# Two-layer attention block: modulation with raw fp32 weights stationary, and its chunks moved

## The chip, the cores and the metric

One core of one Trainium2 chip runs one launch of the kernel. The metric is the device time of the launch in microseconds (us). Everything below is fp32 work: a product is made either from fp32r (reduced precision) high and low parts, or from plain fp32 operands.

## The reference

Two blocks follow each other. The first has an AB layer (latent attention and grouped-query attention) and a CD layer (window attention and a short convolution), over 512 tokens of width 1024 with a context of 256 tokens. The second has an even and an odd layer. Only the first block has the modulation that is changed here:

```python
sc, scc = jax.nn.silu(c), jax.nn.silu(c_ctx)          # [1024] each
for i in range(2):                                    # the AB layer, the CD layer
    mod   = sc  @ mod_w[i] + mod_b[i]                 # mod_w[i]: [1024, 3072]
    mod_c = scc @ mod_w[i] + mod_b[i]
    # shift, scale, gate = three parts of 1024
    # h = rmsnorm(x) * (1 + scale) + shift ;  x = x + gate * (mix @ w_out)
```

So each layer multiplies a 1024 x 3072 matrix by two vectors (one for the tokens, one for the context). Shift and scale are needed before the layer's input projections, the gate only at its output projection.

## The kernel before

The weights of each layer's modulation are laid out as 12 chunks of 256 columns, 1 MB each: chunks 0 to 3 are the shift, 4 to 7 the scale, 8 to 11 the gate. A chunk arrives as two loads of 512 KB. With two layers there are 24 chunks.

*A chunk before.* ScalarE casts each 128x512 quarter of the chunk to its high part and VectorE subtracts for the low part: four casts and four subtractions. TensorE holds the vectors stationary (`sc4`, 128x4: high and low parts of the two vectors) and streams the weights: 16 matmuls of 256 columns. The result is a row block, [4, 256]. A second pair of small fp32 matmuls (L348, stationary [5, 128], two columns moving) turns rows into per-feature columns, sums the high and low parts and adds the bias. The gates stay rows: they are spilled, summed with two matmuls of 512 columns (`gate_sum`, L361), spilled again, and broadcast over the partitions by a DMA (`gate_bc`, L368).

*Where the chunks run.* The eight shift and scale chunks of layer 0 run in `start` (L641), which also normalises and transposes the tokens; their loads rotate through four buffers (`mraw`). `ab_first` (L690), the first projection, takes each feature block as it is finished. The eight shift and scale chunks of layer 1 (`mods`) and the four gate chunks of layer 0 run among the projections of the AB layer (latents, queries, gates). The four gate chunks of layer 1 run as fillers inside the window attention of the CD layer.

*Order.* The kernel is written for a tile framework. The order in which functions are traced gives priority; the framework then lays out each engine's instruction list ahead of time, with a timeline of its own, so that work that is ready fills gaps. Tiles of one name rotate through a fixed number of buffers in trace order: `raw` has three of 512 KB, shared by all weight loads. `pace` (L613) spreads units of filler work over the items of an attention; `hook` ties work to one item. All weight loads and most spills are issued from SP's queue. PSUM bank F is single: projections, modulation and, late in the grouped-query attention, attention outputs use it in turn.

Of the kernel before, what the change touches and what calls it, by code (L numbers as in the profile page):

```python
# [9 lines left out]
F32 = mybir.dt.float32  # L10
# [19 lines left out]
class Kern:  # L30
# [69 lines left out]
    def setup(self, stack):  # L100
# [8 lines left out]
        self.grow_d, self.gsum_d = ([self.dram.tile([n, 1024], F32, name=f"g{n}row{l}_d") for l in range(2)] for n in (5, 2))  # L109
# [6 lines left out]
        self.sel2 = c.tile([5, 2], F32, name="sel2")  # L116
        nc.scalar.dma_start(out=self.sel2, in_=I["sel"])
# [17 lines left out]
    def rstd(self, ms, n):  # L135
        """ms [128, n] mean squares -> (ms + eps)^-0.5"""
# [4 lines left out]
    def split(self, src, hi, lo):  # L141
        """hi, lo (fp32r) of a fp32 AP (PSUM or SBUF)"""
# [16 lines left out]
    def silu2(self, ps, out):  # L159
        """out = 2*silu(ps)"""  # L160
# [4 lines left out]
    def head_norm(self, ps, H, d):  # L165
        """ps PSUM [128, T, H*d] -> normalised fp32 SBUF [128, T, H, d] (no gain)"""
# [18 lines left out]
    def rope(self, out, xn, C, S, r0, rot):  # L185
        """out = xn*C plus the rotary part on [r0, r0+rot), half-split pairs; C [128, T, d], S [128, T, rot]"""
# [12 lines left out]
    def gain_heads(self, out, xn, g):  # L199
        """out = xn*g over [128, T, H, d]"""  # L200
# [9 lines left out]
    def weights(self, ap):  # L210
        """ap DRAM [128, nk, n] -> [(k0, hi, lo)] pieces in fp32r"""
# [48 lines left out]
    def proj_feat(self, out, X, W, c0, t0, n):  # L260
        """feature-major block: out PSUM [128, n] = W[:, c0:c0+128]^T @ X[:, t0:t0+n]"""
# [20 lines left out]
    def feat(self, X, W, t=512):  # L282
        """feature blocks of a chunk over t tokens: yields (b, PSUM [128, n], t0, n)"""
# [9 lines left out]
    def load_silu_c(self):  # L293
# [7 lines left out]
        self.split(self.sc, self.sc4[:, :, 0:2], self.sc4[:, :, 2:4])  # L301

    def mod_load(self, layer, ch, pool):
        """the loads of a mod chunk, ahead of mod_first"""
        rows = self.tl(pool, [5, 256], "rows", 4)
        self.nc.scalar.dma_start(out=rows[4:5, :], in_=self.I["mod_b"][layer:layer + 1, 256 * ch:256 * ch + 256])
        raws = []
        for k in (0, 4):
            raws.append(self.tl(pool, [128, 4, 256], "mraw", 4))
            self.nc.sync.dma_start(out=raws[-1], in_=self.I["mod_w"][layer, ch][:, k:k + 4, :])  # L310
        return rows, raws

    def mod_first(self, ld, pool):
        """rows [5, 256] (x, ctx hi parts, lo parts, bias) of a loaded mod chunk"""
        nc = self.nc
        rows, raws = ld
        p = self.B()
        for kk in range(8):
            if kk % 2 == 0:
                hi, lo = (self.tl(pool, [128, 2, 256], x, 5, F32R) for x in ("mhi", "mlo"))  # L320
                self.split(raws[kk // 4][:, kk % 4:kk % 4 + 2, :], hi, lo)
            for j, w in enumerate((hi, lo)):
                nc.tensor.matmul(out=p[0:4, 0:256], lhsT=self.sc4[:, kk, :], rhs=w[:, kk % 2, :], start=kk + j == 0,
                                 stop=kk == 7 and j == 1)
        nc.vector.tensor_copy(out=rows[0:4, :], in_=p[0:4, 0:256])
        return rows, self.sel2

    def mod_rows(self, layer, ch):
        """rows [5, 256] (x, ctx hi parts, lo parts, bias) of mod chunk ch"""
        nc = self.nc  # L330
        W = self.weights(self.I["mod_w"][layer, ch])
        rows = self.T4([5, 256])
        nc.scalar.dma_start(out=rows[4:5, :], in_=self.I["mod_b"][layer:layer + 1, 256 * ch:256 * ch + 256])
        p = self.B()
        for k0, hi, lo in W:
            for k in range(hi.shape[1]):
                kk = k0 + k
                nc.tensor.matmul(out=p[0:4, 0:256], lhsT=self.sc4[:, kk, :], rhs=hi[:, k, :], start=kk == 0, stop=False)
                nc.tensor.matmul(out=p[0:4, 0:256], lhsT=self.sc4[:, kk, :], rhs=lo[:, k, :], start=False, stop=kk == 7)
        nc.vector.tensor_copy(out=rows[0:4, :], in_=p[0:4, 0:256])  # L340
        return rows, self.sel2

    def mod_cols(self, layer, ch, rs):
        """per-feature columns modT[layer][:, 2*ch + b, (x, ctx)]; the scales with one added"""
        rows, sel = rs
        p = self.B()
        for b in range(2):
            self.nc.tensor.matmul(out=p[:, 2 * b:2 * b + 2], lhsT=rows[:, 128 * b:128 * b + 128], rhs=sel)  # L348
        self.nc.vector.tensor_scalar(out=self.modT[layer][:, 2 * ch:2 * ch + 2, :].rearrange("p b e -> p (b e)"),
                                     in0=p[:, 0:4], scalar1=1.0, scalar2=1.0 if ch >= 4 else 0.0,  # L350
                                     op0=ALU.mult, op1=ALU.add)

    def gate_rows(self, layer, chs):
        """rows [5, 256] of the gate's chunks, spilled"""
        for h in chs:
# [1486 lines left out]
```

## Time and profile before

| | |
|---|---|
| time, median of 3 runs | 1550.29 us (1546.9 to 1552.76) |
| profiled execution, span of its instructions | 1546.3 us |
| TensorE (PE) busy | 1486.4 us, 96% |
| weight loads of TensorE (PEld) busy | 1373.0 us, 89% |
| VectorE (DVE) busy | 1036.5 us, 67% |
| ScalarE (ACT) busy | 846.5 us, 55% |
| GpSimd (POOL) busy | 546.9 us, 35% |
| HBM read and written | 144.06 MB and 22.28 MB |

The profile shows one execution, of which only the span is given, not a time of its own: the runs lie 0.6 to 6.5 us above the span, the median 4.0. Busy time of PE counts the modelled end of each matmul, so neighbours overlap. PEclk is the granted TensorE clock as a share of full speed: 1.00 is 2.4 GHz and 0.50 is 1.2 GHz. L followed by a number is a line of the kernel.

### The profile page before, as it was taken

The numbers are of one execution on the slowest core, as the hardware profiler recorded it, in microseconds if no ns is written. First come the engines' busy times: TensorE is split into PE (matmuls) and PEld (weight loads), VectorE is DVE, ScalarE is ACT, GpSimd is POOL, SyncE is SP. The second block draws the span as 40 slices with busy tenths as digits, with TensorE's granted clock in tenths as the row PEclk, the third lists the DMA queues.
The fourth block names the chain that finished last, engine by engine and source line by source line (L and its number), as shares of the span: only waits on it lengthen the run. The fifth ranks groups of instructions, "written<-read, shape, count | busy, mean of one in ns | idle before, by whom it ended". The sixth has DMA issues, their size and how long they took to land.

```text
span 1546.3 us, 28606 instructions
## 1 busy us (share of the span) xinstructions
PE 1486.4 (96%) x10760; PEld 1373.0 (89%) x10760; DVE 1036.5 (67%) x2121; ACT 846.5 (55%) x1759; POOL 546.9 (35%) x652
## 2 busy tenths in 40 slices
PE   6899999989999999999999999999999999999998
PEld 3799788877998999888889889998899999998998
DVE  6777887889886477777755458986544465565444
ACT  6545555689996154565643446557433544455322
POOL 1533533567674033232421434444201334443000
PEclk8999999999999999999999999999999999999999
DMA  8344564121221332322234222124334321223423
GB/s 304 121 128 120 183 203 162 45 103 33 63 70 31 146 121 71 101 96 86 93 115 145 80 96 82 66 86 137 116 103 143 119 94 57 82 69 132 148 90 110
DMA packets 60685, 168.20 MB, mean 109 GB/s; under 512 B 9890, under 2 KB 18530, under 8 KB 60546
## 3 DMA queue, kind: packets, MB, share of 16 engines
q1 hardware_dynamic: 54768, 163.52, 31.8%
q10 hardware_dynamic: 5778, 2.84, 0.7%
q8 instruction: 85, 1.39, 0.4%
q14 instruction: 54, 0.44, 0.1%
HBM read 144.06 MB, written 22.28 MB: 108 GB/s over the span
## 4 chain that ended last, share of the span: by engine, by line
PE 79%; DVE 8%; DMA 5%; ACT 3%; issue 2%; POOL 2%; SPq 0%; ACTq 0%; DVEq 0%; POOLq 0%
PE A L240 17%; PE A L238 17%; PE A L239 17%; PE B L524 3%; PE F L238 3%; PE F L239 3%; PE F L240 3%; PE F L595 2%; PE B L238 2%; PE B L239 2%; PE B L240 2%; DVE wl L232 1%; PE B L996 1%; PE B L388 1%; PE B L1168 1%
## 5 line engine op out<-in xcount | busy, mean ns | idle before, releaser
L229 ACT CAST wh<-raw 128x512 fp32r<-128x512 f32 (+1 forms) x388 | 232.4, 616 | 237.8 <-PE A L240 166.9
L232 DVE TENSOR_TENSOR wl<-raw,wh 128x512 fp32r<-128x512 f32 (+1 forms) x320 | 233.4, 744 | 93.9 <-ACT wh L229 90.7
L481 POOL TENSOR_SCALAR P<-P,s 128x768 f32<-128x768 f32 (+3 forms) x192 | 152.8, 801 | 176.4 <-DVE s L1264 33.4
L144 DVE TENSOR_TENSOR PTl<-B,PTh 128x512 fp32r<-128x512 f32 (+2 forms) x208 | 127.9, 633 | 47.7 <-ACT PTh L143 35.0
L232 POOL TENSOR_TENSOR wl<-raw,wh 128x512 fp32r<-128x512 f32 x68 | 90.9, 1338 | 158.3 <-ACT wh L229 132.0
L138 POOL TENSOR_TENSOR s8f<-s8f,mhalf 128x4 f32<-128x4 f32 (+2 forms) x53 | 61.5, 1161 | 227.3 <-DVE s8f L137 119.7
L238 PE MATMUL A<-wh,mh 128*128 128x256 f32 x480 | 136.5, 285 | 2.9 <-ACT mh L143 2.9
L143 ACT CAST PTh<-B 128x512 fp32r<-128x512 f32 (+2 forms) x208 | 108.2, 545 | 53.8 <-PE B L524 27.1
L239 PE MATMUL A<-wl,mh 128*128 128x256 f32 x480 | 136.0, 284 | 0.0
L240 PE MATMUL A<-wh,g 128*128 128x256 f32 x408 | 115.7, 285 | 1.2 <-DVE g L144 1.2
L240 PE MATMUL A<-wh,h2l 128*128 128x256 f32 x384 | 108.7, 286 | 2.5 <-DVE h2l L408 2.5
L238 PE MATMUL A<-wh,h4h 128*128 128x256 f32 x384 | 109.5, 286 | 1.0 <-ACT h4h L407 0.8
L240 PE MATMUL A<-wh,h4l 128*128 128x256 f32 x384 | 108.7, 285 | 0.5 <-DVE h4l L408 0.5
L238 PE MATMUL A<-wh,h2h 128*128 128x256 f32 x384 | 108.9, 284 | 0.3 <-ACT h2h L407 0.3
L239 PE MATMUL A<-wl,h4h 128*128 128x256 f32 x384 | 108.7, 284 | 0.0
L239 PE MATMUL A<-wl,h2h 128*128 128x256 f32 x384 | 108.6, 283 | 0.0
L238 PEld LDWEIGHTS A<-wh,mh 128*128 128x128 f32 x480 | 91.9, 192 | 4.3 <-ACT mh L143 3.3
L239 PEld LDWEIGHTS A<-wl,mh 128*128 128x128 f32 x480 | 92.0, 192 | 0.1
L524 PE MATMUL B<-ident,P 128*128 128x128 f32 x592 | 86.2, 274 | 4.5 <-DVE PTl L144 2.4
L240 PEld LDWEIGHTS A<-wh,g 128*128 128x128 f32 x408 | 78.0, 192 | 1.7 <-DVE g L144 1.7
L490 ACT ACTIVATE P<-A,s 128x768 f32<-128x768 f32 (+1 forms) x96 | 73.2, 766 | 7.4 <-DVE s L488 4.7
L524 PEld LDWEIGHTS B<-ident,P 128*128 128x128 f32 x592 | 67.5, 141 | 9.2 <-POOL P L481 2.5
(515 smaller groups left out, 4914.8 us busy)
## 6 DMA issues: line engine op xcount, KB each, us to landing
raw<-mod_w SPq DMA_DIRECT2D x32, 512.0 KB
raw<-even_w SPq DMA_DIRECT2D x32, 512.0 KB
raw<-odd_w SPq DMA_DIRECT2D x32, 512.0 KB
raw<-cd_w SPq DMA_DIRECT2D x26, 512.0 KB
mraw<-mod_w SPq DMA_DIRECT2D x16, 512.0 KB
raw<-w_ple_gate SPq DMA_DIRECT2D x16, 512.0 KB
raw<-ab_wg SPq DMA_DIRECT2D x8, 512.0 KB
raw<-ab_wo SPq DMA_DIRECT2D x8, 512.0 KB
```

Source lines behind the costliest of these rows:

```text
L138: self.nc.gpsimd.tensor_tensor(out=ms, in0=ms, in1=self.mhalf[:, 0:n], op=ALU.pow)
L143: self.nc.scalar.copy(out=hi, in_=src)
L144: self.nc.vector.tensor_tensor(out=lo, in0=src, in1=f32(hi), op=ALU.subtract)
L229: nc.scalar.copy(out=hi, in_=r)
L232: eng.tensor_tensor(out=lo, in0=r, in1=f32(hi), op=ALU.subtract)
L238: mm(out=out, lhsT=xh, rhs=wh, start=start, stop=False)
L239: mm(out=out, lhsT=xh, rhs=wl, start=False, stop=False)
L240: mm(out=out, lhsT=xl, rhs=wh, start=False, stop=stop)
L481: self.nc.gpsimd.tensor_scalar(out=P, in0=P, scalar1=s, scalar2=0.0, op0=ALU.mult, op1=ALU.add)
L490: nc.scalar.activation(out=P[:, u, :], in_=S[:, u, :], func=AF.Exp, bias=m[:, u:u + 1], scale=1.0, accum_out=s[:, u:u + 1])
L524: nc.tensor.transpose(out=pt[:, j, u, :], in_=b, identity=self.ident)
L595: nc.tensor.matmul(out=O, lhsT=vst(e, j), rhs=pts[j // 2][w][:, j % 2], start=w + j == 0, stop=w == 1 and j == nk - 1)
```

## The change

The weights of a chunk are no longer cast or split. TensorE takes each raw fp32 block of 128x128 as the stationary operand and streams the two vectors past it (two columns), so the result stands per feature at once: 16 fp32 matmuls for a chunk. One VectorE addition from PSUM adds the bias, which is loaded once as columns (`mb`, with one added for the scales). The gates are now columns as well (`modT` has 24 instead of 16), and `gate_bc` makes the broadcast by a VectorE copy, four transposes and a ScalarE copy for each half.

In `start` the loads of the eight chunks rotate through ten buffers instead of four. The four gate chunks of layer 0 and the eight shift and scale chunks of layer 1 leave the projections of the AB layer: twelve units are paced over the 24 items of its grouped-query attention. The four gate chunks of layer 1 leave the window attention: they are traced behind the last token pair of the AB layer's output projection. Outside `start`, chunks load into the shared `raw` buffers, and each matmul reads the load's own buffer.

```diff
 def setup(self, stack):
-        self.sc4 = c.tile([128, 8, 4], F32R, name="sc4")
+        self.mb = c.tile([128, 2, 24], F32, name="mb")
+        nc.scalar.dma_start(out=self.mb, in_=I["mod_bt"])
+        nc.vector.tensor_scalar(out=self.mb[:, :, 8:16], in0=self.mb[:, :, 8:16], scalar1=1.0, scalar2=None, op0=ALU.add)
-        self.modT = [c.tile([128, 16, 2], F32, name=f"modT{l}") for l in range(2)]
+        self.modT = [c.tile([128, 24, 2], F32, name=f"modT{l}") for l in range(2)]
...
-    def mod_load(self, layer, ch, pool):
...
-    def mod_first(self, ld, pool):
...
-    def mod_rows(self, layer, ch):
...
-    def mod_cols(self, layer, ch, rs):
...
-    def gate_rows(self, layer, chs):
...
-    def gate_sum(self, layer, bank="F"):
...
+    def mod_load(self, layer, ch, pool=None):
+        raws = []
         for k in (0, 4):
+            raws.append(self.tl(self.rawp, [128, 4, 256], "raw") if pool is None else self.tl(pool, [128, 4, 256], "mraw", 10))
             self.nc.sync.dma_start(out=raws[-1], in_=self.I["mod_w"][layer, ch][:, k:k + 4, :])
+        return raws
+    def mod_cols(self, layer, ch, raws):
         p = self.B()
         for b in range(2):
+            for k in range(8):
+                self.nc.tensor.matmul(out=p[:, 2 * b:2 * b + 2], lhsT=raws[k // 4][:, k % 4, 128 * b:128 * b + 128],
+                                      rhs=self.sc[:, k, :], start=k == 0, stop=k == 7)
+        self.nc.vector.tensor_tensor(out=self.modT[layer][:, 2 * ch:2 * ch + 2, :],
+                                     in0=p[:, 0:4].rearrange("p (b e) -> p b e", b=2),
+                                     in1=self.mb[:, layer, 2 * ch:2 * ch + 2].unsqueeze(2).to_broadcast([128, 2, 2]), op=ALU.add)
+    def mods(self, layer, *chs):
+        for ch in chs:
+            self.mod_cols(layer, ch, self.mod_load(layer, ch))
     def gate_bc(self, layer, out, which=0):
-        self.nc.sync.dma_start(out=out[which], in_=self.gsum_d[layer][which:which + 1, :].to_broadcast([128, 1024]))
+        for h in range(2):
+            t = self.T4([128, 512])
+            self.nc.vector.tensor_copy(out=t.rearrange("p (b f) -> p b f", b=4),
+                                       in_=self.modT[layer][:, 16 + 4 * h:20 + 4 * h, which].unsqueeze(2).to_broadcast([128, 4, 128]))
+            p = self.B("T")
+            for b in range(4):
+                c = slice(128 * b, 128 * b + 128)
+                self.nc.tensor.transpose(out=p[:, c], in_=t[:, c], identity=self.ident)
+            self.nc.scalar.copy(out=out[which][:, 512 * h:512 * h + 512], in_=p)
 def start(self, X, mp, xp):
-            self.mod_cols(0, order[j], self.mod_first(lds[j], mp))
+            self.mod_cols(0, order[j], lds[j])
 def run(self):
-            self.ab_lat(X, L, latg, lambda: self.mods(0, 1))
-            self.mods(2, 3)
+            self.ab_lat(X, L, latg)
...
-            self.mods(4, 5)
...
-            self.mods(6, 7)
...
-            self.gate_rows(0, range(4))
-            self.gate_sum(0)
...
+        def more():
+            for layer, ch in [(0, ch) for ch in range(8, 12)] + [(1, ch) for ch in range(8)]:
+                self.mods(layer, ch)
+                yield
+        self.pace(items, more(), 12)
         self.hook(items, 0, lambda: during(0))
...
             def after(t):
...
+                if t == 4:
+                    self.mods(1, 8, 9, 10, 11)
...
             def rest():
                 for g in range(2):
                     yield from self.cd_conv(Xx, cp, cw, g, cvs[g])
-                    for h in (2 * g, 2 * g + 1):
-                        self.gate_rows(1, (h,))
-                        yield
...
-                self.gate_sum(1)
-                yield
...
-            self.pace(items, ru, 21)
+            self.pace(items, ru, 16)
```

## Rows read from the trace of the kernel before

**Rows 1.** The profile's page: busy time of TensorE; the chain's shares by engine.

```profile
PE 1486.4 (96%) x10760; PEld 1373.0 (89%) x10760; DVE 1036.5 (67%) x2121; ACT 846.5 (55%) x1759; POOL 546.9 (35%) x652
...
PE 79%; DVE 8%; DMA 5%; ACT 3%; issue 2%; POOL 2%; SPq 0%; ACTq 0%; DVEq 0%; POOLq 0%
```

**Rows 2.** Busy time by stretch of the span; the first line names the columns.

```profile
core 0: us, PE busy (x) PEld busy (x) DVE busy (x) ACT busy (x) POOL busy (x), PEclk, DMA share, GB/s
0.00:76.00 76.00, 57.22 (x360) 43.94 (x360) 52.16 (x100) 45.57 (x86) 26.71 (x26) 0.91 0.62 211
76.00:244.00 168.00, 162.62 (x1142) 144.51 (x1142) 132.70 (x322) 89.46 (x180) 64.32 (x68) 0.99 0.53 170
244.00:400.00 156.00, 144.01 (x1038) 130.63 (x1039) 129.65 (x233) 126.05 (x292) 93.50 (x114) 1.00 0.18 63
400.00:490.00 90.00, 88.50 (x683) 83.32 (x681) 72.27 (x136) 80.39 (x193) 60.71 (x83) 1.00 0.20 60
...
640.00:780.00 140.00, 139.68 (x820) 118.40 (x819) 103.87 (x238) 88.21 (x200) 44.30 (x69) 1.00 0.27 88
```

**Rows 3.** Groups by line and form: the modulation's streamed matmuls, and the start's transposes.

```profile
L338 PE MATMUL F<-wh,sc 128*4 128x256 f32 x128 | 31.1, 281 | 0.4 <-DVE t L340 0.3
...
L388 PE MATMUL F<-ident,t 128*128 128x128 f32 x48 | 9.6, 330 | 2.6 <-DVE s L137 1.5 <-ACT xnT L658 0.9 <-DVE t L379 0.2
```

**Rows 4.** Line 348: engine, form, count; durations in ns, least, median, most.

```profile
L348 PE MATMUL B<-sel,rows x32: 246/246/370, 11.8 to 63.8; 5*128 5x2 f32 x32
```

**Rows 5.** Timeline: start and length in us; first and last of dense runs.

```profile
6.55 0.62 ACT L143 CAST mhi<-mraw 128x512 fp32r<-128x512 f32 x1 [2.31 <-DMA mraw<-mod_w]
...
11.81 0.92 PEld L348 LDWEIGHTS B<-sel,rows 5*128 5x128 f32 x4 [1.00 <-DVE rows L325]
...
38.20 0.28 PE L323 MATMUL B<-mhi,sc 128*4 128x256 f32 x1
...
39.94 0.29 PE L323 MATMUL B<-mlo,sc 128*4 128x256 f32 x1
...
52.49 0.30 PE L238 MATMUL A<-wh,hTh 128*128 128x288 f32 x1
...
56.22 0.29 PE L239 MATMUL A<-wl,hTh 128*128 128x288 f32 x1
...
103.27 0.52 PEld L348 LDWEIGHTS F<-sel,t 5*128 5x128 f32 x4
...
103.80 0.19 PEld L239 LDWEIGHTS A<-wl,hTh 128*128 128x128 f32 x1
...
235.72 1.01 PE L364 MATMUL F<-t,sel 5*2 5x512 f32 x2
...
236.66 0.73 PE L240 MATMUL A<-hTh,wl 128*128 128x512 f32 x2
```

**Rows 6.** The chain that ended last, in order of time, in the start.

```profile
34.90 6.75 DMA mraw<-mod_w
...
76.58 0.39 PE A L238
```

**Rows 7.** The page's 40 slices of 38.7 us: what the DMA engines moved.

```profile
GB/s 304 121 128 120 183 203 162 45 103 33 63 70 31 146 121 71 101 96 86 93 115 145 80 96 82 66 86 137 116 103 143 119 94 57 82 69 132 148 90 110
```

**Rows 8.** Short stretches, columns as in rows 2.

```profile
29.30:32.70 3.40, 2.25 (x18) 1.72 (x17) 3.40 (x9) 2.53 (x5) 0.00 (x0) 1.00 0.68 170
...
490.10:493.50 3.40, 1.72 (x12) 1.43 (x12) 0.69 (x1) 1.97 (x5) 2.09 (x3) 1.00 0.08 19
...
560.00:580.00 20.00, 16.89 (x130) 16.45 (x129) 16.27 (x31) 10.72 (x21) 6.92 (x10) 0.91 0.46 149
```

**Rows 9.** Timeline of SP's queue and TensorE behind the AB layer's output projection.

```profile
521.56 6.63 SPq L222 DMA_DIRECT2D raw<-cd_w  x3
...
562.38 0.28 PE L238 MATMUL A<-wh,h1ch 128*128 128x256 f32 x1
```

**Rows 10.** Groups by line and form: VectorE's copies of 128x512 in the start.

```profile
L658 DVE COPY xnT<-F 128x512 f32<-128x512 f32 x6 | 4.1, 679 | 1.3 <-PE F L388 1.3
```

More of the change, by code (lines that the diff above doesn't have):

```diff
@@ L108, in setup @@
         self.dram = ent(self.pool("dram", space=DRAM))
-        self.grow_d, self.gsum_d = ([self.dram.tile([n, 1024], F32, name=f"g{n}row{l}_d") for l in range(2)] for n in (5, 2))
         self.rot_d = [self.dram.tile([128, 4, 2, n], F32, name=f"rot{n}_d") for n in (16, 32)]
@@ L115, in setup @@
         nc.vector.memset(self.mhalf, -0.5)
-        self.sel2 = c.tile([5, 2], F32, name="sel2")
-        nc.scalar.dma_start(out=self.sel2, in_=I["sel"])
         self.sc = c.tile([128, 8, 2], F32, name="sc")
-        self.sc4 = c.tile([128, 8, 4], F32R, name="sc4")
+        self.mb = c.tile([128, 2, 24], F32, name="mb")
+        nc.scalar.dma_start(out=self.mb, in_=I["mod_bt"])
+        nc.vector.tensor_scalar(out=self.mb[:, :, 8:16], in0=self.mb[:, :, 8:16], scalar1=1.0, scalar2=None, op0=ALU.add)
         self.ng = c.tile([128, 2, 8], F32, name="ng")
         nc.scalar.dma_start(out=self.ng, in_=I["norm_g_2"])
-        self.modT = [c.tile([128, 16, 2], F32, name=f"modT{l}") for l in range(2)]
+        self.modT = [c.tile([128, 24, 2], F32, name=f"modT{l}") for l in range(2)]
     def gain_row(self, pool, name, tag, scale=None):
@@ L300, in load_silu_c @@
         nc.vector.tensor_tensor(out=self.sc, in0=th, in1=ct, op=ALU.mult)
-        self.split(self.sc, self.sc4[:, :, 0:2], self.sc4[:, :, 2:4])
-    def mod_load(self, layer, ch, pool):
-        rows = self.tl(pool, [5, 256], "rows", 4)
-        self.nc.scalar.dma_start(out=rows[4:5, :], in_=self.I["mod_b"][layer:layer + 1, 256 * ch:256 * ch + 256])
+    def mod_load(self, layer, ch, pool=None):
         raws = []
         for k in (0, 4):
-            raws.append(self.tl(pool, [128, 4, 256], "mraw", 4))
+            raws.append(self.tl(self.rawp, [128, 4, 256], "raw") if pool is None else self.tl(pool, [128, 4, 256], "mraw", 10))
@@ L310, in mod_load @@
             self.nc.sync.dma_start(out=raws[-1], in_=self.I["mod_w"][layer, ch][:, k:k + 4, :])
-        return rows, raws
-    def mod_first(self, ld, pool):
[L315 to L326, printed above, removed]
@@ L328, in mod_rows @@
-    def mod_rows(self, layer, ch):
[L330 to L341, printed above, removed]
@@ L343, in mod_cols @@
-    def mod_cols(self, layer, ch, rs):
-        rows, sel = rs
+        return raws
+    def mod_cols(self, layer, ch, raws):
         p = self.B()
         for b in range(2):
[L348 to L351, printed above, removed]
@@ L353, in gate_rows @@
-    def gate_rows(self, layer, chs):
-        for h in chs:
-            rows, _ = self.mod_rows(layer, 8 + h)
-            self.nc.sync.dma_start(out=self.grow_d[layer][:, 256 * h:256 * h + 256], in_=rows)
-    def gate_sum(self, layer, bank="F"):
-        for h in (0, 512):
-            rows, r, p = self.T4([5, 512]), self.T4([2, 512]), self.B(bank)
-            self.nc.sync.dma_start(out=rows, in_=self.grow_d[layer][:, h:h + 512])
-            self.nc.tensor.matmul(out=p[0:2, :], lhsT=self.sel2, rhs=rows)
-            self.nc.scalar.copy(out=r, in_=p[0:2, :])
-            self.nc.sync.dma_start(out=self.gsum_d[layer][:, h:h + 512], in_=r)
@@ L740, in ab_q, with ab_lat @@
         return q
-    def mods(self, *chs):
-        for ch in chs:
-            self.mod_cols(1, ch, self.mod_rows(1, ch))
-    def ab_lat(self, X, L, latg, between):
+    def ab_lat(self, X, L, latg):
         nc = self.nc
@@ L768, in ab_lat @@
                 self.split(p, L[0][:, 2 * c:2 * c + 2, 128 * t:128 * t + 256], L[1][:, 2 * c:2 * c + 2, 128 * t:128 * t + 256])
-            if c == 0:
-                between()
     def ab_gates(self, X, ch, out):
@@ L1770, in layout @@
     d["ct"] = A(np.stack([g["c"][0], g["c_ctx"]], -1).reshape(8, 128, 2).transpose(1, 0, 2))
-    d["mod_w"], d["mod_b"] = np.stack([chunks(w) for w in g["mod_w"]]), A(g["mod_b"])
+    d["mod_w"] = np.stack([chunks(w) for w in g["mod_w"]])
+    d["mod_bt"] = A(g["mod_b"].reshape(2, 24, 128).transpose(2, 0, 1))
     ab = g["ab_w_in"][0]
@@ L1809, in layout @@
     d["rope_ab"] = A(rope.reshape(4, 128, -1).transpose(1, 0, 2))
-    d["sel"] = np.array([[1, 0], [0, 1], [1, 0], [0, 1], [1, 1]], f)
     neg = f(-1e30)
```

## The prediction

> **What bounds the kernel now.** I read the page first: TensorE is busy 96% of the span, and the chain that ended last spends 79% on it [rows 1]. So the question for every stage is whether TensorE has idle time there. The busy times by stretch answer it [rows 2]. From 76 to 244 us, where twelve modulation chunks run among the projections, TensorE is busy 162.6 of 168 us, and from 640 to 780, with four more chunks, 139.7 of 140: both are bound by it. From 244 to 400 (mostly the grouped-query attention) it is busy 144.0 of 156, with ScalarE at 126.1 and VectorE at 129.7. In the start, 0 to 76, it is idle 18.8 us, and its mean clock is 0.91. There VectorE's subtractions and late loads stand on the chain [rows 6]. The page's slices show that the first 38.7 us move 304 GB/s, that is 11.8 MB, about all that the start needs (16 chunk loads and 6 token tiles of 512 KB, 11.5 MB) [rows 7]. So the start has its data by about 40 us, yet the first dense projection behind it begins at 76.6 [rows 6].
>
> **The price of a chunk on TensorE.** Before: 16 matmuls of 256 columns, which follow each other every (39.94 - 38.20)/15 = 0.116 us [rows 5], 1.86 us, and the small matmuls of line 348, 0.53 us from 103.27 to 103.80 [rows 5]: 2.4 us. The cast and subtraction of four quarters are on other engines.
>
> After: 16 fp32 matmuls with 128 stationary columns and two moving columns. Line 348 is that form but for its five rows. Its group in the start has 32 records for eight chunks of two matmuls, so an fp32 matmul is two loads of weights and two matmuls [rows 4]. Four such loads take 0.52 us at the full clock; one is 0.19 long, so the next begins (0.52 - 0.19)/3 = 0.11 us later [rows 5]. With two columns to stream, nothing covers the load. A chunk is 32 x 0.111 = 3.6 us. At the half clock four loads took 0.92 us, between 0.20 and 0.23 each [rows 5]; I take 0.213, so 6.8 us a chunk. Rows of one length, five or 128 rows tall, cost alike: 0.19 us is the duration of a 128x128 load too [rows 5]. Thus TensorE's work rises by 1.2 us a chunk at best, some 29 us for 24 chunks, and the change pays only where it moves work into idle time.
>
> The Trainium skill has another price, in FP8 and Floating Point Precision, section TensorE Precision Notes: true fp32 takes four passes through the array. If each were a load of its own, a chunk would be 64 x 0.111 = 7.1 us, an estimate by that page, and the sum some 85 us higher. The two records for each matmul in this trace decide against four loads.
>
> **Which clock the start gets.** From 29.3 to 32.7 us TensorE is busy 2.25 of 3.4 us, mostly with transposes and the short matmuls of line 348, and a half-clock stretch follows; from 490.1 to 493.5 it is busy less, 1.72 us, but with 256-column matmuls, and the full clock stays (1.00 from 400 to 490 and in that row) [rows 8, 2]. The new start is load after load with two columns each, nearer to the first. I take the half clock for its chunks.
>
> **The sum, part by part.**
>
> *Start.* The first chunk is there at 6.55 us [rows 5]. Then TensorE has work without a gap: eight chunks, 48 transposes [rows 3] at 0.11 or 0.213 us, 144 projection matmuls of 288 columns at (56.22 - 52.49)/28 = 0.133 us [rows 5], 19.2 us, and about 4 us of last scaling and splitting, estimated. Half clock: 6.5 + 54.5 + 10.2 + 19.2 + 4 = 94.4 us; full clock: 6.5 + 28.6 + 5.3 + 19.2 + 4 = 63.6. Against 76.6 that is +18 or -13. I take +16, since the projections that mix in may raise the clock for a few chunks. The ten buffers bring nothing: the data is early already.
>
> *76 to 244 us.* Twelve chunks leave: 12 x 1.86 = 22.3, eight times 0.53 = 4.2, and two sums of 0.94 us each (235.72 to 236.66) [rows 5], 1.9. That is 28.4 us of an engine that is full; 48 casts and subtractions go from ScalarE and VectorE, which ends some of its waits. I take -30 (bounds -27 and -33, from the 5.4 us idle there [rows 2]).
>
> *Attention, 244 to 400.* Twelve chunks come: 43 us at the full clock, 82 at the half. The cover is TensorE's idle time. Busy time says 12.0 us; 1038 matmuls at 0.116 would fill 120 us, so it is 36 at most [rows 2, 5]. I take 20, between them, since the 512-column matmuls take longer than 0.116. The stage grows by 43 - 20 = 23, and by 4 more for bursts in which the clock falls: +27 (bounds +7 and +70; the upper end needs every burst at half clock). Behind the units in SP's queue and in the `raw` rotation stand the gates of the second group and the output projection's weights, which were prefetched early; their casts move to 400 to 490, where ScalarE is busy 80.4 of 90 [rows 2]. Twelve casts are within the remaining 9.6 us: 0, at most +7.
>
> *Behind the output projection.* Four chunks, 14.4 us. Before, this place had idle time: 3.1 of 20 us from 560 to 580, at 0.91 clock [rows 8], because the last pair's normalisation is awaited; I count 3. But the chunks hold the `raw` buffers until their matmuls are done, two of three each, while the weights of the CD layer, loaded from 521 on before, wait behind them in the rotation; their projection began at 562.4 [rows 9]. I add 5 for loads and clock. With the four chunks gone from 640 to 780 (4 x 1.86 + 2 x 0.94 = 9.3) that is 14.4 - 3 + 5 - 9.3 = +7 (bounds 0 and +20).
>
> *Gates.* Three broadcasts: 24 transposes at 0.11, 2.6 us, six VectorE copies of 0.68 [rows 10] and as many on ScalarE, taken alike. In series this is 10.8; they run ahead of their use beside the splits: +2. The single additions of bias lie beside other work.
>
> Sum: +16 - 30 + 27 + 7 + 2 = +22. On the span of 1546.3 this gives 1568.3; the median of the runs lies 4.0 above the span, so **1572 us**, 1.4% slower.
>
> **Rivals.**
>
> *The clock stays full.* If loads back to back hold the clock, the start is -13, the attention +23, the place behind the output projection +3: -13 - 30 + 23 + 3 + 2 = -15, so 1535 us, faster. For it: TensorE never idles in the new start. Against it: the stretch at 29.3 [rows 8]. The other stages then sum to -2, so a gain over 0.5% (8 us) needs the start below 70.6 us, which is a chunk under (70.6 - 35)/8 = 4.4 us. The Trainium skill has this rule in TensorE: Matmul & The Clock Gate, Part 1: activity releases the throttle and idleness brings it back. Its Part 4 says that transposes do not count as busy in the same way; the trace agrees as far as the row at 29.3 goes, and no row here shows long runs of weight loads.
>
> *The attention hides the chunks.* If the cover is 36 us, the attention grows by 7 + 4 = 11: the sum is +6, 1556 us, no change that can be told. For it: single idle times are many there, and the units wait for nothing but their loads. Against it: each engine's order is laid out ahead, and TensorE at 88.5 of 90 us in the stage behind it [rows 2] can take nothing over.
>
> *The chunks also stall the attention.* If most bursts run at the half clock, and the single bank F makes attention outputs wait for them, the attention grows by 45 instead of 27, and behind the output projection the loads cost 15 instead of 5: +50, 1600 us.
>
> **How the numbers follow.** Forecast 0.48, full clock 0.25, hidden 0.15, stalled 0.12. A measurement of this kernel can tell about 0.5%, 1542.5 to 1558.0. Faster: most of the full-clock case and a little of the hidden one, 0.24. Same: most of the hidden case, and the edges of its neighbours, 0.16. Slower: the forecast, the stalled case and the hidden one's upper part, 0.60. The forecast's own range, from its bounds without the far ends, is 1558 to 1588. For 8 in 10 the range must take in most of the full-clock and stalled cases: 1528 to 1602.
>
> **What would show it.** Right: the loads of the new chunks about 0.21 us apart in the start, a clock of 0.5 in most of its stretches up to 60 us, the dense projections beginning after 85 us; the stage from them to the attention about 30 us shorter; the stage to the output projection some 25 us longer with TensorE near full. The prediction is wrong if the start's clock is near 1.00 and the projections begin before 70 us, if a load costs other than 0.11 us at the full clock, or if the attention grows by less than 12 us.

## The result, and the profile after

The changed kernel takes **1609.95 us** (median of 4 runs, 1604.1 to 1614.65); the kernel before, on the same chip, 1548.6. The ratio is 1.0383, with a 95% interval of 1.0359 to 1.0408: slower by 61 us. The forecast was 1572 with a range of 1528 to 1602, so sign and direction were right and the size was outside the range.

The page of the changed kernel, to be read against [rows 1]: TensorE's busy time has grown by 81.4 us and its share to 97%.

```profile
PE 1567.8 (97%) x11096; PEld 1482.2 (92%) x11096; DVE 969.8 (60%) x2015; ACT 798.8 (50%) x1664; POOL 523.3 (32%) x652
...
PE 80%; DVE 5%; DMA 4%; ACT 2%; issue 2%; POOL 2%; ACTq 0%; DVEq 0%; POOLq 0%
```

Only 336 matmuls came on balance; at 0.11 us each, the price at the full clock, they are 37 us. Most of the other 44 us is work done slower. Where it sits is seen in the stretches of the changed kernel (columns as in [rows 2]; the bounds are its own stages):

```profile
core 0: us, PE busy (x) PEld busy (x) DVE busy (x) ACT busy (x) POOL busy (x), PEclk, DMA share, GB/s
0.00:92.00 92.00, 84.06 (x450) 84.04 (x451) 27.62 (x67) 29.37 (x54) 19.83 (x29) 1.00 0.46 174
92.00:226.00 134.00, 131.79 (x938) 123.86 (x937) 98.25 (x244) 63.42 (x130) 57.27 (x64) 1.00 0.35 118
226.00:428.00 202.00, 193.04 (x1252) 182.64 (x1251) 114.67 (x214) 107.23 (x244) 79.28 (x99) 0.81 0.31 105
428.00:541.60 113.60, 111.69 (x850) 104.91 (x850) 92.06 (x172) 99.94 (x239) 74.64 (x101) 1.00 0.19 60
541.60:614.60 73.00, 70.38 (x584) 69.97 (x583) 32.44 (x55) 19.88 (x35) 6.53 (x8) 0.98 0.27 91
614.60:647.00 32.40, 29.63 (x161) 28.85 (x159) 17.19 (x34) 11.44 (x22) 9.32 (x10) 0.58 0.43 145
```

The grouped-query attention (226 to 428) has a mean clock of 0.81, the four chunks behind the output projection (614.6 to 647) 0.58. The 1.00 of the first row is not to be trusted: the trace's first record of the clock lies at 73.7 us (a later run with an earlier one, warm2, shows 0.50 at the same spacing). The spacing of the pairs (a pair is a weight load and its matmul) shows the half clock, as in the first row of the next view, TensorE's timeline in the changed kernel (start, length): 32 pairs in 7.06 us.

```profile
7.94 7.06 PE L314 MATMUL B<-sc,mraw 128*128 128x2 f32 x32 [7.94 <-DMA mraw<-mod_w]
...
249.81 0.39 PE L434 MATMUL A<-kA,qs 128*128 128x512 f32 x1
250.04 0.39 PE L435 MATMUL A<-kB,qs 128*128 128x512 f32 x1
...
251.86 4.35 PE L314 MATMUL F<-sc,raw 128*128 128x2 f32 x32
256.07 0.77 PE L434 MATMUL A<-kA,qs 128*128 128x512 f32 x1
256.64 0.63 PE L435 MATMUL A<-kB,qs 128*128 128x512 f32 x1
257.07 0.41 PE L434 MATMUL A<-kA,qs 128*128 128x256 f32 x1
```

The same view shows a chunk in the attention. Score matmuls (queries by keys) of 512 columns follow each other in 0.23 us ahead of it (249.81 to 250.04). One chunk of 32 pairs runs without a gap. Behind it the same matmuls are 0.57 and 0.43 us apart. The short stretches around it give the clock: it falls to 0.50 within the chunk and stays there 6.8 us, while TensorE is busy in every us of the three.

```profile
251.20:254.60 3.40, 3.40 (x34) 3.40 (x32) 2.63 (x6) 2.17 (x5) 1.20 (x1) 1.00 0.02 5
254.60:261.40 6.80, 6.80 (x32) 6.61 (x32) 5.26 (x11) 2.27 (x6) 5.19 (x4) 0.50 0.51 154
261.40:264.80 3.40, 3.40 (x31) 3.40 (x32) 2.73 (x8) 1.89 (x6) 1.81 (x3) 1.00 0.01 2
```

Behind the output projection SP's queue, in the changed kernel, shows three chunk loads early and five late, and the CD layer's weights only behind those, where before they came from 521.56 on, 41 us ahead of their use [rows 9]:

```profile
574.37 6.57 SPq L306 DMA_DIRECT2D raw<-mod_w  x3
...
618.39 20.02 SPq L306 DMA_DIRECT2D raw<-mod_w  x5
639.79 7.91 SPq L221 DMA_DIRECT2D raw<-cd_w  x4
```

And TensorE there (timeline): a wait of 2 us, the last two chunks at 0.21 us a pair, and the first projection of the CD layer at 646.95, 32 us behind the last matmul of the output projection. Before, it followed at once (562.38) [rows 9].

```profile
614.57 0.28 PE L239 MATMUL A<-wh,mixl 128*128 128x256 f32 x1
614.69 0.50 PE L314 MATMUL F<-sc,raw 128*128 128x2 f32 x4
...
622.12 0.90 PE L353 MATMUL B<-ident,t4f 128*128 128x128 f32 x2 [2.00 <-DVE t4f L344]
...
632.93 6.83 PE L314 MATMUL F<-sc,raw 128*128 128x2 f32 x32
640.01 7.07 PE L314 MATMUL F<-sc,raw 128*128 128x2 f32 x32 [0.25 <-DVE modT L316]
646.95 0.56 PE L237 MATMUL A<-wh,h1ch 128*128 128x256 f32 x1
```

The same stages of every run with its whole program, in us, from TensorE's timelines of the profiled executions. The bounds are the start of: the first 256-column projection of the AB layer, its last gate projection (512 columns), the last value matmul of the latent attention, the last matmul of the output projection, the first and the last projection matmul of the CD layer's tokens, and the last matmul.

| run | start | AB projections | attention | output projection | gap | CD projections and window attention | rest |
|---|---|---|---|---|---|---|---|
| before | 76.6 | 165.3 | 249.6 | 70.7 | 0.1 | 230.6 | 749.0 |
| after | 91.8 | 134.3 | 315.4 | 73.0 | 32.4 | 212.3 | 747.5 |
| wide64 | 91.7 | 134.4 | 288.3 | 72.1 | 27.5 | 210.1 | 747.1 |
| warm | 74.0 | 134.1 | 284.8 | 72.5 | 27.1 | 209.7 | 749.9 |
| warm2 | 90.8 | 133.6 | 318.6 | 72.7 | 32.4 | 211.2 | 752.7 |
| attn0 | 91.2 | 134.3 | 246.7 | 73.8 | 27.0 | 210.9 | 750.0 |
| thin64 | 91.4 | 134.0 | 263.4 | 73.2 | 21.2 | 211.8 | 750.2 |
| cd_t0 | 72.2 | 134.6 | 285.0 | 88.8 | 0.1 | 216.4 | 748.7 |
| place | 91.7 | 202.1 | 247.1 | 72.8 | 0.1 | 251.6 | 744.0 |
| oldnew | 75.2 | 137.3 | 301.0 | 72.2 | 27.1 | 213.0 | 752.1 |
| best | 70.0 | 168.2 | 250.0 | 70.6 | 0.1 | 229.7 | 737.9 |
| best96 | 65.1 | 163.6 | 250.6 | 71.1 | 0.1 | 231.1 | 746.3 |

From before to after: +15 in the start, -31 in the AB projections, +66 in the attention, +2 in the output projection, +32 in the gap, -18 in the CD layer, -1.5 in the rest. That is 65 us, as the spans of the two profiled executions differ (1611.6 and 1546.3 us); the medians of all runs differ by 61.

### The profile page after: what moved, and what is told of

The parts are those of the page before. It is cut to its first block, busy times and chain, and to the rows that moved or that the text cites. A ratio compares the mean times of both kernels' runs of the same rounds, so it can differ in the third digit from the quotient of the medians.

```text
span 1611.6 us, 28847 instructions
## 1 busy us (share of the span) xinstructions
PE 1567.8 (97%) x11096; PEld 1482.2 (92%) x11096; DVE 969.8 (60%) x2015; ACT 798.8 (50%) x1664; POOL 523.3 (32%) x652
## 4 chain that ended last, share of the span: by engine, by line
PE 80%; DVE 5%; DMA 4%; ACT 2%; issue 2%; POOL 2%; ACTq 0%; DVEq 0%; POOLq 0%
PE A L237 16%; PE A L239 16%; PE A L238 16%; PE B L489 4%; PE F L314 4%; PE F L237 3%; PE F L238 3%; PE F L239 3%; PE F L560 2%; PE B L237 1%; PE B L238 1%; PE B L239 1%; PE B L954 1%; PE A L434 1%; PE B L353 1%
## 5 line engine op out<-in xcount | busy, mean ns | idle before, releaser
L228 ACT CAST wh<-raw 128x512 fp32r<-128x512 f32 (+1 forms) x324 | 196.0, 615 | 232.3 <-PE A L239 150.1
L231 DVE TENSOR_TENSOR wl<-raw,wh 128x512 fp32r<-128x512 f32 (+1 forms) x256 | 187.7, 746 | 104.6 <-ACT wh L228 102.7
L446 POOL TENSOR_SCALAR P<-P,s 128x768 f32<-128x768 f32 (+3 forms) x192 | 144.4, 758 | 228.6 <-DVE s L457 59.1
L231 POOL TENSOR_TENSOR wl<-raw,wh 128x512 fp32r<-128x512 f32 x68 | 91.4, 1345 | 158.7 <-ACT wh L228 132.0
L489 PE MATMUL B<-ident,P 128*128 128x128 f32 x592 | 93.8, 288 | 1.2 <-DVE PTl L143 0.7
L453 DVE TENSOR_REDUCE s<-A 128x1 f32<-128x768 f32 (+1 forms) x80 | 71.5, 897 | 19.3 <-PE A L435 16.7
L314 PEld LDWEIGHTS F<-sc,raw 128*128 128x128 f32 x512 | 79.8, 247 | 2.0 <-ACT t L473 1.6
L314 PE MATMUL F<-sc,raw 128*128 128x2 f32 x512 | 78.9, 287 | 1.7 <-ACT t L473 1.4
```

Of the source, the lines that this page charges most:

```text
L228: nc.scalar.copy(out=hi, in_=r)
L231: eng.tensor_tensor(out=lo, in0=r, in1=f32(hi), op=ALU.subtract)
L314: self.nc.tensor.matmul(out=p[:, 2 * b:2 * b + 2], lhsT=raws[k // 4][:, k % 4, 128 * b:128 * b + 128], rhs=self.sc[:, k, :], start=k == 0, ...
L446: self.nc.gpsimd.tensor_scalar(out=P, in0=P, scalar1=s, scalar2=0.0, op0=ALU.mult, op1=ALU.add)
L453: nc.vector.tensor_reduce(out=m, in_=S, axis=AX.X, op=ALU.max, negate=True)
L489: nc.tensor.transpose(out=pt[:, j, u, :], in_=b, identity=self.ident)
```

## The experiments

Theory A: the missing size is the clock; matmuls of two columns behind each weight load let it fall although TensorE never idles. Theory B: the chunks stall their neighbours by waits, on the single bank F, the shared `raw` buffers and their loads. Theory C: it is only TensorE's added work. The names of the runs are those of the table.

### wide64: the same weight loads, 64 columns moving

```diff
-        self.sc = c.tile([128, 8, 2], F32, name="sc")
+        self.scw = c.tile([128, 78], F32, name="scw")
+        nc.vector.memset(self.scw, 0.0)
+        self.sc = self.scw[:, 0:16].rearrange("p (k e) -> p k e", e=2)
...
-                self.nc.tensor.matmul(out=p[:, 2 * b:2 * b + 2], lhsT=raws[k // 4][:, k % 4, 128 * b:128 * b + 128],
-                                      rhs=self.sc[:, k, :], start=k == 0, stop=k == 7)
+                self.nc.tensor.matmul(out=p[:, 64 * b:64 * b + 64], lhsT=raws[k // 4][:, k % 4, 128 * b:128 * b + 128],
+                                      rhs=self.scw[:, 2 * k:2 * k + 64], start=k == 0, stop=k == 7)
...
```

> The changed kernel with one difference: each modulation matmul moves 64 columns instead of 2 (the same table of the two vectors, read 64 columns wide with zeros behind it; the first two result columns are used as before). The count of weight loads, the loads from HBM, their buffers, the PSUM bank and the order are the same. Theory A (the half clock is what the forecast lacked: two-column matmuls let the clock fall although TensorE is never idle): the clock stays near 1.00 through the chunks, pairs follow each other every 0.11 us everywhere, the start ends near 64 us instead of 92, the grouped-query attention is 30 to 40 us shorter than in the changed kernel, the place behind the output projection 10 to 16 us shorter: about 1540 us. Theory B (the chunks stall the attention by bank F and by the raw buffers): nothing of that changes, 1605 to 1615 us. Theory C (TensorE's work simply grows with the chunks): the wider matmuls cost more, 1610 us or above.

Measured: 1582.68 us (1577.86 to 1584.74), 1.0198 of before (1.0174 to 1.0223), some 27 below the changed kernel. The attention fell by 27 us, with a clock of 0.96. The same chunk as above, in this kernel's timeline, takes 3.68 us, and the scores behind it are 0.32 and 0.23 us apart:

```profile
251.81 3.68 PE L316 MATMUL F<-scw,raw 128*128 128x64 f32 x32
255.30 0.48 PE L436 MATMUL A<-kA,qs 128*128 128x512 f32 x1
255.62 0.39 PE L437 MATMUL A<-kB,qs 128*128 128x512 f32 x1
255.85 0.28 PE L436 MATMUL A<-kA,qs 128*128 128x256 f32 x1
```

More columns made the kernel faster, so C falls. But B's expectation of no change fails too, and the total is 43 us above what A alone expected: the start did not move (91.7), the attention is still 39 us above before, and the gap is 27.5.

### bench and bench2: the price and the clock of a pair by itself

In both, 192 pairs of weight load and matmul without a wait between; in the first behind 20 dense fp32 matmuls of 512 columns, in the second behind 192 pairs with two columns, which leave the clock at one half.

```diff
+        for n in (2, 8, 16, 32, 64, 96, 128):
+            q = self.B()
+            for k in range(20):
+                nc.tensor.matmul(out=q[:, 0:512], lhsT=self.ident, rhs=mv, start=k == 0, stop=k == 19)
+            for b in range(2):
+                for r in range(6):
+                    for k in range(8):
+                        nc.tensor.matmul(out=p[:, n * b:n * b + n], lhsT=w[:, k, 128 * b:128 * b + 128], rhs=mv[:, 0:n],
+                                         start=r + k == 0, stop=r == 5 and k == 7)
...
```

> Computes nothing of the reference. Seven times: 20 fp32 matmuls of 512 columns, then 96 fp32 matmuls (192 pairs of weight load and matmul) whose moving operand is 2, 8, 16, 32, 64, 96 and 128 columns wide, all from SBUF, without any wait between them. Theory A: with 2 columns the pairs start 0.11 us apart and within a few us 0.21 apart, with a granted clock of 0.5; above some width, 32 to 96, the clock stays 1.00 and the pairs 0.11 us apart. Theories B and C (the clock falls only where TensorE waits for something): 0.11 us apart at every width up to 64, a clock of 1.00 throughout.

> Computes nothing of the reference. Five times: 20 fp32 matmuls of 512 columns, 96 fp32 matmuls with 2 columns moving (which bring the clock to one half), then 96 with 64, 96, 128, 192 and 256 columns. Theory A (64 columns hold the full clock but do not lift the half one, as the start of the kernel with 64 columns suggests): at 64 the clock stays at 0.5 and the pairs 0.21 us apart; from some width on, 96 to 256, it rises to 1.00 within a few us. Rival (the start was slow for another reason): at 64 columns, too, the clock rises within a few us.

Timeline of bench, TensorE; the moving operand's width is in the form (128x2, 128x32 and so on):

```profile
25.99 36.44 PE L1400 MATMUL D<-mv,w 128*128 128x2 f32 x192
...
199.09 35.59 PE L1400 MATMUL D<-mv,w 128*128 128x32 f32 x192
...
254.05 21.55 PE L1400 MATMUL D<-mv,w 128*128 128x64 f32 x192
...
331.26 21.60 PE L1400 MATMUL D<-mv,w 128*128 128x128 f32 x192
```

Two stretches of bench, the pairs with two and with 64 columns (columns of the view: us, PE busy, PEld busy, DVE busy, POOL busy, PEclk, DMA share, GB/s):

```profile
25.99:62.40 36.41, 36.41 (x194) 36.40 (x192) 0.69 (x1) 0.00 (x0) 0.57 0.00 1
...
254.10:275.50 21.40, 21.40 (x194) 21.40 (x193) 0.69 (x1) 0.00 (x0) 1.00 0.00 1
```

Timeline of bench2, TensorE, behind the half clock; the 64-column pairs have a clock of 0.50 from their start to their end:

```profile
65.55 41.20 PE L1403 MATMUL D<-mv,w 128*128 128x64 f32 x192
...
161.69 24.00 PE L1403 MATMUL D<-mv,w 128*128 128x96 f32 x192
239.12 24.54 PE L1403 MATMUL D<-mv,w 128*128 128x128 f32 x192
```

With 64 columns a chunk's 32 pairs cost 21.55 / 6 = 3.6 us, the forecast's price. With two they take 36.44 us, at a mean clock of 0.57 and with TensorE busy throughout; there is nothing to wait for. And the same 64-column pairs take 21.55 us behind the full clock and 41.20 behind the half one: in these runs they kept whichever they found. That would explain why wide64's start stayed slow; the next two runs try it.

### warm and warm2: the clock raised ahead of the start

```diff
+        z = self.T4([128, 512])
+        nc.vector.memset(z, 0.0)
+        p = self.B()
+        for k in range(6):
+            nc.tensor.matmul(out=p, lhsT=z[:, 0:128], rhs=z, start=k == 0, stop=k == 5)
         self.load_silu_c()
...
-            self.mod_cols(0, order[j], lds[j])
+            self.mod_cols(0, order[j], lds[j], 192 if j < 3 else 64)
```

The last change, and 64 columns elsewhere, are in warm alone.

> The changed kernel with 64 columns moving, six fp32 matmuls of 512 columns on zeros ahead of the first chunk, and 192 columns moving for the first three chunks of the start, while data still arrive (nine load buffers instead of ten in the start). Theory A (the start runs at the half clock because nothing in it lifts the clock that the launch begins with; 64 columns only hold it): clock 1.00 and pairs 0.11 us apart in the start, the first dense projection at 62 to 70 us instead of 91.7, and the whole 22 to 30 us below the 1583 us of the kernel with 64 columns alone: about 1556 us. Rival (fp32 weight loads in the start are slow for another reason, the DMA's writes into the buffers for one): the first dense projection stays near 92 us, 1583 us.

> The changed kernel with the six fp32 matmuls of 512 columns ahead of the first chunk and nothing else (two columns moving, nine load buffers in the start). Theory A: the clock rises in the first us and falls again within the first chunks; pairs 0.21 us apart for most of the start, the first dense projection at 85 to 91 us. Rival (the clock that the launch begins with is all that counts): 64 to 75 us.

Measured: warm 1561.63 us (1558.4 to 1568.64), 1.0085 of before (1.0059 to 1.0111); warm2 1618.56 in one run. In warm the start is 74.0 us, longer than expected by 4; TensorE idles 6.8 us in it, and the first three chunks' wider matmuls cost more. In warm2 it is 90.8. Its dense matmuls brought the clock up, so its fall is recorded (a mean of 0.64 from 8 to 20 us); two stretches of warm2's start show 0.50 with TensorE busy throughout and 98 pairs in 20 us, the spacing that the changed kernel has there:

```profile
20.00:40.00 20.00, 20.00 (x98) 20.00 (x97) 7.42 (x20) 7.45 (x18) 2.57 (x4) 0.50 1.02 407
40.00:60.00 20.00, 20.00 (x98) 20.00 (x97) 2.07 (x5) 2.55 (x5) 0.55 (x1) 0.50 0.04 17
```

So a raised clock is not enough, and neither are 64 columns: the start needs both. (Whether 64 columns in the first three chunks would do, once the clock is raised, was not tried; best96 below has 96.) Warm's grouped-query attention has a clock of 1.00, and shows what is left without the clock's part:

```profile
208.00:378.00 170.00, 159.46 (x1245) 150.00 (x1243) 113.36 (x213) 105.60 (x243) 79.86 (x98) 1.00 0.35 122
```

### attn0 and thin64: what the attention hides

attn0 leaves the twelve chunks of the attention out of wide64; thin64 keeps their loads and takes two of eight blocks.

```diff
 attn0
-                self.mods(layer, ch)
+                if ch == 8 or ch == 0:
+                    nc.vector.memset(self.modT[layer][:, 16 if ch else 0:24 if ch else 16, :], 0.5)
                 yield
...
 thin64
-            self.mod_cols(layer, ch, self.mod_load(layer, ch))
+            self.mod_cols(layer, ch, self.mod_load(layer, ch), (0, 4))
```

> The changed kernel with 64 columns moving and without the twelve chunks of the attention (loads, matmuls and additions left out; constants stand in their place). It measures how much of them the attention hid. Theory A2 (nothing to hide them in): the attention is as long as in the kernel before, 245 to 252 us from the last gate projection to the last value matmul, so that of the chunks' 43 us of TensorE at most 5 to 10 were hidden. Theory B2 (the attention itself was made slower, by what the chunks displace in queues and buffers): 225 to 240 us, shorter than before, because other work left it with them.

> The changed kernel with 64 columns moving, and of each chunk outside the start only four of its sixteen matmuls (two of eight feature blocks): three quarters of the products of those sixteen chunks are left out, but every load, every buffer, every visit to bank F and every addition stays. Theory A2 (with the clock kept up, what is left of the attention's growth is TensorE's own work, for which there was hardly any idle time to hide it in): the attention, 288.4 us from the last gate projection to its last value matmul with the full chunks, loses some 30 of its remaining 39 us of growth: 255 to 262 us; behind the output projection 17 us instead of 27.5. Theory B (bank F, the raw buffers and the loads): the attention stays at 278 us or more, and the place behind the output projection at 24 or more.

Measured, one run each: attn0 1540.22 us, its attention 246.7 (expected by A2: 245 to 252); thin64 1551.53, its attention 263.4 (255 to 262, just missed). Stretches of attn0, grouped-query and latent attention:

```profile
225.50:358.80 133.30, 122.31 (x870) 109.39 (x869) 109.30 (x202) 105.70 (x244) 79.82 (x98) 1.00 0.18 65
358.80:472.20 113.40, 111.13 (x848) 104.52 (x846) 91.81 (x172) 99.82 (x239) 75.20 (x102) 1.00 0.20 60
```

TensorE's idle time in the grouped-query attention is 11.0 us without chunks (133.3 - 122.3) and 10.5 in warm with all twelve (170.0 - 159.5). The gaps were not filled. From attn0 to warm the attention grows by 38.1 us for 43 of chunk work: 5 were hidden. With loads, buffers and bank F in place but a quarter of the matmuls, thin64 loses 25 of wide64's 42 us over attn0. So the length of the attention follows TensorE's work in the main, and B accounts for little: of the 16.7 us that are left in thin64 the quarter's matmuls are 10.8, and TensorE's waits for the chunks' loads come to 5.6 (1.3 in warm). In the gap B holds in part: three quarters of the matmuls gone, 10.8 us at the full clock, saved 6.3 (21.2 us are between the two expectations), and a stretch of thin64 shows TensorE busy 12.3 of 21 us there:

```profile
562.00:583.00 21.00, 12.32 (x65) 11.21 (x63) 16.00 (x33) 10.61 (x21) 9.47 (x10) 0.64 0.66 222
```

### cd_t0: the last four chunks traced earlier

```diff
-                if t == 4:
+                if t == 0:
                     self.mods(1, 8, 9, 10, 11)
```

> The kernel with 64 columns and the matmuls ahead (1561.6 us), with the four gate chunks of layer 1 traced behind the first token pair of the output projection instead of the last. Theory B for this place (the projection of the CD layer stands in TensorE's order behind four chunks whose loads wait for raw buffers, and its own weights wait behind those): the loads come during the output projection, the gap between it and the CD layer's projection shrinks from 27 us to at most 8, the output projection itself grows by 12 to 15: together 5 to 12 us less, 1550 to 1557 us. Theory A alone (only TensorE's work and its clock): what leaves one place comes back in the other, 1558 to 1563 us.

Measured: 1554.57 us (1552.08 to 1557.26; 10 runs), 1.0035 of before (1.0024 to 1.0045), 7 below warm. That is B's range and not A's. The output projection grows by 16 us (12 to 15 expected), the gap is gone, and the projection of the CD layer follows at once again. Together the two shrink from 99.6 to 88.9 us. Stretches of warm (output projection, gap) and of cd_t0 (both in one):

```profile
492.90:565.40 72.50, 69.88 (x584) 69.47 (x583) 32.46 (x55) 19.89 (x35) 6.55 (x9) 0.98 0.26 92
565.40:592.50 27.10, 24.00 (x160) 23.01 (x159) 16.93 (x34) 11.38 (x22) 9.79 (x10) 0.80 0.50 177
...
491.90:580.70 88.80, 86.67 (x721) 86.11 (x720) 39.28 (x69) 25.56 (x46) 6.56 (x8) 0.96 0.40 133
```

The 10.7 us are not all waiting. TensorE idles 2.1 us instead of 5.7; the clock (what PEclk lacks to 1.00, times the length) takes 3.6 instead of 6.9; and 23 matmuls fewer run there. In the CD layer 6.7 us come back (209.7 to 216.4), 4.5 of them idle time of TensorE; 1.8 of the gain over warm lie in the start, which has nothing to do with it. So the early loads close the gap, but the wait in it is a few us, and only about 4 of the 10.7 reach the end.

### place and oldnew: each half of the change by itself

place has the new method at the old places; oldnew the old method at the new ones.

```diff
 place
+            self.ab_lat(X, L, latg, lambda: self.mods(1, 0, 1))
+            self.mods(1, 2, 3)
...
+            self.mods(0, 8, 9, 10, 11)
...
-        self.pace(items, more(), 12)
...
 oldnew
+                self.gate_rows(0, (h,))
...
+                self.mods(ch)
...
+        self.pace(items, more(), 12)
...
+                if t == 4:
+                    self.gate_rows(1, range(4))
+                    self.gate_sum(1)
```

> The changed kernel with its chunks put back to the places of the kernel before (among the AB layer's projections, and four in the window attention); the method stays the new one. Theory A: the attention returns to its old length; the projections from 77 to 244 us keep twelve chunks that now cost 43 us at the full clock and 82 at the half, instead of 28: the stage is 15 to 50 us longer than before, with a lower clock, and the whole 1585 to 1615 us. Theory B: the attention's stalls are gone, the rest is the dearer chunk at the full clock: start +15, projections +15, window attention +5, some 1585 us.

> The kernel before with its method (cast, split, weights streamed 256 columns wide) and only the move: twelve chunks paced over the grouped-query attention, four behind the AB layer's output projection. Theory A: the move does no harm by itself, since streamed weights hold the clock: the projections are 30 us shorter, the attention 8 to 20 us longer, the place behind the output projection about 10 us longer and the window attention 9 us shorter: 1525 to 1545 us, with a clock near 1.00 from 244 to 400. Theory B (bank F and the raw buffers): attention 40 us longer or more, the place behind the output projection 25 us longer: 1570 us or above.

Measured: place 1618.87 us (1615.55 to 1622.57), 1.0444 of before; oldnew 1583.2 (1581.42 to 1584.17), 1.0205 (1.0186 to 1.0223). place is just above A's range: the AB projections are 37 us longer than before, at a clock of 0.86, and the CD layer is 21 longer. oldnew is a miss for A, which expected 1525 to 1545, and every figure of B came: 1570 or above, the attention 40 longer or more, the gap 25 longer (27.1). Its attention takes 301.0 us, 51 longer, for 28 us of TensorE's work:

```profile
212.60:400.70 188.10, 162.67 (x1098) 139.36 (x1097) 148.70 (x269) 132.77 (x293) 83.54 (x97) 0.92 0.35 113
```

TensorE idles 25 us there and the clock is 0.92. VectorE and ScalarE have 148.7 and 132.8 us of work, where attn0's have 109.3 and 105.7: the casts and subtractions moved along. By TensorE's waits there, 22.6 of the 25 us end on VectorE or ScalarE, among them 1.9 in which attention outputs wait for the modulation in bank F, and 1.5 end on a DMA. So TensorE itself waited little for B's bank F and loads. That the moved casts are the larger part is argued from these rows, not tried, and loads that come late to the casts are not excluded. Both halves of the change cost, then, and not as a sum: +67 and +31 alone, +61 together.

### best and best96: the new method in the start alone

The kernel before, with warm's start (eight load buffers); in best96 with 96 columns instead of 192 for the first three chunks.

```diff
-            self.mod_cols(0, order[j], self.mod_first(lds[j], mp))
+            self.mod_cols1(0, order[j], lds[j], 192 if j < 3 else 64)
```

> The kernel before with the new method in the start alone (eight chunks, with 64 and 192 columns moving and the six matmuls ahead, as in the run beside it); the other sixteen chunks by the old method at their old places. Theory A: the start ends 7 to 14 us earlier, nothing else changes: 1536 to 1545 us against 1551, faster than both kernels. If the start stays at the half clock: 1565 us. If the old places' casts were late for another reason than the start: 1551 us.

> The kernel before with the new method in the start alone (1531.3 us), with 96 columns instead of 192 for its first three chunks. If those chunks' extra columns cost time there: 2 to 5 us faster, 1527 to 1529 us. If they only fill the wait for the data: 1531 us. If the clock then falls in the start: 1535 to 1545 us.

Measured: best **1531.25 us** (1528.49 to 1536.17), 0.9886 of before (0.9865 to 0.9907); best96 1532.27 (1531.47 to 1533.96), 0.989 (0.9875 to 0.9905). Both beat both kernels, best by more than was expected (1536 to 1545); the narrower matmuls of best96 bring no more in the median. best96's start is 65.1 us, 11.5 shorter than before and 1.5 from the forecast's sum at the full clock, 63.6; it has idle time left, and the clock holds:

```profile
0.00:65.00 65.00, 60.74 (x460) 55.80 (x461) 30.46 (x69) 28.88 (x54) 21.56 (x29) 1.00 0.70 251
```

The two are alike in their medians although best's start is 5 us longer. In best's profiled execution 11 us came off behind the CD layer ("rest"), where nothing was changed; no run here explains it. So the start accounts for 11.5 of best96's 18 us below before, and for 7 of best's 19.

## Why the prediction was wrong

**The step that failed is the attention, +27 us, and in it two terms.** Measured: +66. The term "4 more for bursts in which the clock falls" is 30.6 us (after 315.4, warm 284.8). The cover of 20 us is 5. With the 43 us of work at the full clock, which stood, and 2.9 by which attn0 lies below before: 43 - 5 + 30.6 - 2.9 = 65.7.

The clock's row was read rightly for the start and then not carried to the attention, though a chunk there is the same run of 32 pairs. The falls were priced at 4 us without a row for them. But in the chunk at 251.86 the clock fell, and then the attention's own matmuls, too, ran at half speed behind it (the scores above). The bound of +70 held this case and was set aside as "every burst at half clock". The Trainium skill, TensorE: Matmul & The Clock Gate, Part 1, has activity release the throttle. If the profile's busy time is taken for activity, this case does not agree: in warm2 the clock was 0.50 in two stretches in which TensorE was busy 20.00 of 20.00 us.

The cover was read from busy time against the sum of spacings, 12 to 36 us. The idle time was there and stayed: it is as long with the chunks as without. The hidden rival (1556) falls with it.

**Behind the output projection**, +7: measured, +32 in the gap and -18 in the CD layer, +14. The term "5 for loads and clock" was too small by the clock above all: the mean clock in the gap is 0.58, and the chunks' 128 pairs are 27.3 us at 0.213 instead of 14.4, 12.9 more, while TensorE idles 2.8 of the 32.4 us. The clock is not all of it: in wide64, at 0.80, the gap is still 27.5, and cd_t0 shows some wait for the loads. The return in the CD layer was 18 and not 9.3, as its stretches before and after show: 109 matmuls fewer, some 30 of which now run in the gap, and 3.8 us less idle time.

```profile
562.40:793.00 230.60, 224.87 (x1388) 195.74 (x1387) 169.94 (x362) 132.21 (x284) 77.32 (x103) 0.99 0.27 89
...
647.00:859.20 212.20, 210.26 (x1279) 185.95 (x1279) 143.41 (x316) 114.83 (x249) 60.03 (x90) 0.99 0.23 78
```

**What held.** The price of a pair, two loads for a matmul, 0.11 us at the full clock and 0.213 at the half one. The start, +16: +15.2, and by the half clock (warm2's rows). The AB projections, -30: -31. The gates, +2: +2.3 in the output projection. The casts moved into the latent attention, 0: +1. TensorE near full in the attention: 304.7 of 315.6 us busy.

**The rivals.** The full clock (1535) was wrong for this kernel, but its sum for the start is what best96 then showed. The stalled attention (1600) was nearest. Its half clock accounts for 30.6 of the 66 us; its bank F, which was not tried by itself, for little. TensorE's waits at bank F behind a chunk, and a chunk's behind the attention, in the changed kernel from 226 to 428 us (us in total, times, longest):

```profile
PE F L237 <- DVE modT L316: 1.4, 1, 1.4
PE F L314 <- ACT t L473: 1.4, 1, 1.4
```

The forecast's own check, "a clock of 0.5 in most of its stretches up to 60 us", could not be read from the column, which had no record there; the spacing had to be taken. The 0.91 of the start before [rows 2] is too high for the same reason: the trace's first record lies at 19.0 us, and ahead of it, from 8.97 to 10.89 us, the streamed matmuls are 0.213 us apart instead of 0.116.

**Left open.** How the gap of 32 us divides between the clock and the wait for the loads; the 11 us of best's rest; and what made oldnew's attention idle.

## What to carry to other kernels

A price that was read at one clock is half a price: if a step can lower the clock, the work behind it is slowed too, and each burst pays again, so the fall belongs into the sum for every place where the step runs. Idle time in a stage is cover only if the moved work can stand in the gaps of that engine's own order; compare the stage with and without the work before counting it. And a change in two parts is worth splitting: here the method paid in the start, used there alone, once its matmuls were made wider and the clock was raised ahead of them.

## What was not expected of the hardware

Making a matmul wider made it faster: 192 pairs took 36.44 us with two columns and 21.55 with 64, and the kernel 1609.95 and 1582.68. The clock depends on what ran before: the same 192 pairs of 64 columns took 21.55 us behind dense matmuls and 41.20 behind the half clock. And where the trace has no record of the clock yet, its column reads 1.00 while the spacing says 0.50.
